# A decoder trunk on one core: MLA's mask and maximum in one VectorE operation, heads spawned ahead of values, words for transposes, a block's eight transposes in one run

## The chip, the core and the metric

The kernel runs on one core of a Trainium2 chip. Its engines work in parallel, each through its own list of instructions: TensorE (PE, matrix products and transposes), VectorE (DVE), ScalarE (ACT), GpSimd (POOL) and SyncE (SP, which issues DMAs). A product's stationary operand is loaded by an instruction of its own (LDWEIGHTS, shown as PEld). [...] The metric is the time of one execution on the device in microseconds, the median of several runs.

## What is computed

A decoder trunk of two layers over 256 positions and a width of 2048, all in float32. Layer 0 mixes with Mamba-2 heads (SSD) and, beside them, 16 heads of latent attention (MLA); layer 1 with stick-breaking attention. After each mixer comes a SwiGLU FFN with 5632 hidden columns, ahead of each sub-layer and at the end an RMSNorm. Most of the change is in MLA:

```python
q = (rms_norm(c_q, q_norm) @ w_uq).reshape(bsz, seq, 16, 128 + 64)
kv = (rms_norm(c_kv, kv_norm) @ w_ukv).reshape(bsz, seq, 16, 128 + 128)
q_nope, q_pe = jnp.split(q, [128], axis=-1)
k_nope, v = jnp.split(kv, [128], axis=-1)
q_pe, k_pe = apply_rope(q_pe, ...), apply_rope(k_rope, ...)
for i in range(2):                       # blocks of 128 query rows
    q0, q1 = i * 128, (i + 1) * 128
    s = (q_nope[q0:q1] @ k_nope[:q1].T + q_pe[q0:q1] @ k_pe[:q1].T) * scale   # per head
    mask = jnp.arange(q1)[None, :] <= jnp.arange(q0, q1)[:, None]
    p = jax.nn.softmax(jnp.where(mask, s, -jnp.inf), axis=-1)
    outs.append(p @ v[:q1])              # per head
```

The Mamba-2 part first runs a causal convolution of four taps with silu over 3072 channels; its outputs feed the scan.

## The kernel before

**Words.** Every float32 operand of a large product is split into two parts in a format that the code calls words (type F32R, 32 bits): ACT casts the high part (L346), DVE subtracts it from the source for the low part (L352), and three products (L460, L462, L463; L905 in the large ones) replace one. In the large layers the products are formed by a scheme of sums of weight blocks: DVE forms differences of weight tiles (L852) in two slots named wsum, and they too are split. Weights stay in SBUF in 12 slots of 8 KB a partition: four wh, six w, two wsum.

**Transposes.** An operand must have its channels on the partitions, so blocks of 128x128 are transposed on PE with an identity as the other operand. `transpose` (L352 to L359) takes `ident_r` if the source is a tile of words, and `ident` if it is f32. The same memory often has two names, one of each type: `twins` (raw and words), `xres` and `xwords` for the residual. Each transpose writes to a PSUM buffer named tr; there are four of them, and four of the accumulators acc. A block of 512 columns has eight transposes (four column tiles, two row tiles); `transpose_split` (L361) and `transpose_plain` (L388) do them in two runs of four into one tr buffer each, one step of the task apart.

**Order.** The order on PE is that of the written code. Beside the projections run tasks: Python generators, of which `yield n` says that the task sleeps for n ticks. A tick comes after each step of a projection's inner loop (a weight row block in both row tiles, six products), and resumes at most two tasks that are due. So a task's instructions stand on PE between products of the running projection. The order on ACT, DVE and POOL is made by a scheduler from priorities: `URGENT` (50000) ahead of the splitting of weights, whose numbers grow as the program goes on.

**MLA.** `mla_group` handles four heads, four times: the rotary part of the queries `qp` (24 products 256 wide), `q` and `k` transposed (48 products 256 wide each), `v` (24 products 512 wide), and then spawns four `mla_head` tasks with first waits of 2, 6, 10 and 14 ticks. A head computes its scores for the two blocks of rows (L1649, L1650) and adds a causal mask by a third product, `identb` with `cmask`, in bf16 (L1651); the scores are in one PSUM buffer `sc` (named at in the profile), 128 columns for the first block of rows and 256 for the second. DVE finds the maximum of each (L1656) and scales it by -scale (L1657); ACT takes the exponent with its sum (L1659); DVE forms the reciprocal (L1661) and scales the probabilities `p` (L1663). Seven ticks after the scores PE transposes three blocks of p (L1667, f32), ACT copies them (L1669), and four ticks later PE forms the output (L1673, L1674).

**Convolution and residual.** `conv` transposes the projected channels, applies the taps on DVE (L1502) and silu on ACT (L1504); four of its six tiles are the scan's x, which is transposed back at L1562. `norm_block` transposes the residual's column blocks j for the next operand; its rank says where it belongs: 100000 and above is the opening of the kernel, 99600 the first block of the last product's end, `URGENT` the blocks that `norm_next` calls.

## Time and profile before

| what | value |
|---|---|
| time, median of 3 runs | 2367.17 us (2367.09 to 2367.3) |
| the profiled execution, whole | 2367.28 us |
| its span in the profile | 2365.2 us |
| TensorE's granted clock in the profiled execution | 0.998 |
| transposes in words of twins | 352 on PE, 39.2 us |
| transposes in words of the residual | 88, 9.7 us |
| f32 transposes: p of MLA, residual, convolution | 48, 7.9 us; 40, 6.4 us; 32, 5.0 us |
| mask products of MLA | 32, 7.0 us |

The span is what the profile covers; the whole execution is 2.1 us longer. The busy times of PE count each product until its end, and since products overlap in a pipeline the distance from one start to the next is shorter than the time of one: busy times of a group on PE are not what the group would cost. A row of a timeline has the start in us, the time until the end of the last of its instructions, the engine, the line, the operation, output and inputs by the program's names, shapes, the count (x4 for four alike in a row), and in brackets the idle time ahead of it and what ended it.

### The profile page before, as it was taken

Reading aid. Unit: us, or ns where it says so; the run is one execution under the profiler, and the core shown is the slowest. Engines: PE = TensorE matmul, PEld = TensorE weight load, DVE = VectorE, ACT = ScalarE, POOL = GpSimd, SP = SyncE. Lnnn points to the kernel's source line nnn. Section 1 sums busy time; section 2 is a strip of 40 time slices with the busy share of each in tenths; the row PEclk is TensorE's granted clock in tenths of the full one; section 3 lists DMA queues with packets and bytes.
Section 4 is the critical chain, followed back from the end, with each engine's and each line's share of the span. In section 5 each row is a group of like instructions: output and inputs, shape, how many; then the busy total and the mean of one; then the engine's idle time right before and its main releaser. Section 6 shows DMA issues by size and latency. Waiting matters only on the chain.

```text
span 2365.2 us, 28220 instructions
## 1 busy us (share of the span) xinstructions
PE 2349.3 (99%) x11082; PEld 1953.9 (83%) x11082; DVE 2001.6 (85%) x1657; ACT 1467.2 (62%) x1486; POOL 215.7 (9%) x273
## 2 busy tenths in 40 slices
PE   9999999999999999999999999999999999999998
PEld 7888888988888888888888888888888888888886
DVE  6776587589998889989887898889997988989895
ACT  6655565566665655566665786776664656556664
POOL 1342001110000000000000020110000000000011
PEclk9999999999999999999999999999999999999999
DMA  7665556445666777777776555557667777767773
GB/s 273 204 194 179 184 196 188 135 142 195 231 203 207 225 217 215 223 219 221 218 241 207 203 182 176 185 175 242 226 203 213 216 228 221 217 214 228 216 253 110
DMA packets 271428, 486.33 MB, mean 206 GB/s; under 512 B 22268, under 2 KB 47488, under 8 KB 271296
## 3 DMA queue, kind: packets, MB, share of 16 engines
q1 hardware_dynamic: 255200, 445.95, 57.3%
q0 software_dynamic: 15232, 37.01, 6.5%
q8 instruction: 87, 1.43, 0.2%
q10 hardware_dynamic: 864, 1.57, 0.2%
q14 instruction: 45, 0.37, 0.0%
HBM read 459.24 MB, written 25.20 MB: 205 GB/s over the span
## 4 chain that ended last, share of the span: by engine, by line
PE 95%; DVE 2%; ACT 2%; issue 1%; DMA 0%; SPq 0%; ACTq 0%; DVEq 0%
PE acc L905 54%; PE acc L460 11%; PE acc L463 11%; PE acc L462 11%; PE tr L357 1%; PE acc L643 1%; PE acc L508 1%; ACT wh L346 1%; PE at L1578 1%; PE acc L510 0%; DVE wsum L852 0%; DVE wsum L352 0%; DVE w L352 0%; PE at L1649 0%; DMA xres<-in_x_dram 0%
## 5 line engine op out<-in xcount | busy, mean ns | idle before, releaser
L352 DVE TENSOR_TENSOR w<-w,wh 128x2048 fp32r<-128x2048 f32 (+2 forms) x399 | 893.4, 2246 | 174.8 <-ACT wh L346 168.4
L905 PE MATMUL acc<-wh,s 128*128 128x512 f32 x3896 | 985.4, 391 | 1.6 <-ACT s L926 1.2
L346 ACT CAST wh<-w 128x2048 fp32r<-128x2048 f32 (+2 forms) x399 | 744.5, 1874 | 322.9 <-PE acc L463 135.3
L905 PEld LDWEIGHTS acc<-wh,s 128*128 128x128 f32 x3896 | 725.5, 188 | 151.0 <-ACT s L926 1.7
L460 PE MATMUL acc<-wh,s 128*128 128x512 f32 (+1 forms) x1168 | 463.4, 397 | 0.1
L463 PE MATMUL acc<-wh,s 128*128 128x512 f32 (+1 forms) x1168 | 452.4, 387 | 0.2 <-DVE s L381 0.2
L462 PE MATMUL acc<-w,s 128*128 128x512 f32 (+1 forms) x1104 | 426.7, 387 | 0.0
L905 PE MATMUL acc<-w,s 128*128 128x512 f32 x1312 | 355.6, 389 | 0.2 <-DVE w L352 0.2
L905 PEld LDWEIGHTS acc<-w,s 128*128 128x128 f32 x1312 | 246.2, 188 | 52.1 <-DVE w L352 0.6
L463 PEld LDWEIGHTS acc<-wh,s 128*128 128x128 f32 x1168 | 219.3, 188 | 46.1 <-DVE s L381 0.6
L460 PEld LDWEIGHTS acc<-wh,s 128*128 128x128 f32 x1168 | 219.4, 188 | 43.6 <-issue 1.7
L462 PEld LDWEIGHTS acc<-w,s 128*128 128x128 f32 x1104 | 207.7, 188 | 40.0 <-issue 1.4
L352 DVE TENSOR_TENSOR wsum<-wsum,wh 128x2048 fp32r<-128x2048 f32 (+1 forms) x103 | 222.1, 2156 | 3.4 <-ACT wh L346 3.3
L346 ACT CAST wh<-wsum 128x2048 fp32r<-128x2048 f32 (+1 forms) x103 | 185.8, 1804 | 57.5 <-PE acc L905 38.4
L1067 POOL DMA_DIRECT2D saved<-s x64 | 55.9, 996 | 1107.0 <-ACT s L1066 1105.8
L346 ACT CAST wh<-lent 128x2048 fp32r<-128x2048 f32 (+1 forms) x62 | 114.6, 1858 | 62.4 <-DMA lent<-in_w_gate_dram 26.0
L352 DVE TENSOR_TENSOR lent<-lent,wh 128x2048 fp32r<-128x2048 f32 (+1 forms) x62 | 137.1, 2217 | 11.6 <-ACT wh L346 11.1
L852 DVE TENSOR_TENSOR wsum<-w,wsum 128x2048 f32<-128x2048 f32 (+1 forms) x54 | 106.7, 1976 | 19.2 <-PE acc L905 16.6
L905 PE MATMUL acc<-wsum,s 128*128 128x512 f32 x380 | 104.6, 390 | 1.4 <-DVE wsum L352 1.4
L905 PEld LDWEIGHTS acc<-wsum,s 128*128 128x128 f32 x380 | 71.2, 188 | 17.1 <-DVE wsum L352 2.2
L926 ACT COPY s<-acc 128x512 f32<-128x512 f32 x88 | 51.6, 588 | 39.1 <-PE acc L905 39.1
L852 DVE TENSOR_TENSOR wsum<-w,w 128x2048 f32<-128x2048 f32 (+1 forms) x36 | 72.6, 2017 | 1.7 <-DMA w<-in_w_qkv_dram 1.7
(280 smaller groups left out, 1966.8 us busy)
## 6 DMA issues: line engine op xcount, KB each, us to landing
w<-in_w_down_dram SPq DMA_DIRECT2D x80, 1024.0 KB, 4.9
w<-in_w_gate_dram SPq DMA_DIRECT2D x76, 1024.0 KB, 5.1
w<-in_w_up_dram SPq DMA_DIRECT2D x76, 1024.0 KB, 5.1
w<-in_w_qkv_dram SPq DMA_DIRECT2D x48, 1024.0 KB, 5.0
w<-in_w_in_dram SPq DMA_DIRECT2D x45, 1024.0 KB, 5.1
w<-in_w_out_even_dram SPq DMA_DIRECT2D x32, 1024.0 KB, 4.9
saved<-s POOLq DMA_DIRECT2D x64, 256.0 KB, 7.3
w<-in_w_out_odd_dram SPq DMA_DIRECT2D x16, 1024.0 KB, 5.0
```

Of the source, the lines that this page charges most:

```text
L346: cast = nc.scalar.copy(hi, src).ins
L352: return nc.vector.tensor_tensor(lo, src, hi.bitcast(F32), op=ALU.subtract).ins
L357: self.nc.tensor.transpose(out.bitcast(F32R), src, self.ident_r)
L460: nc.tensor.matmul(ps[t], hi[:, ts], wh, start=k == 0, stop=False)
L462: slot.used(nc.tensor.matmul(ps[t], hi[:, ts], wl, start=False, stop=False), self.clock)
L463: nc.tensor.matmul(ps[t], lo[:, ts], wh, start=False, stop=k == nk - 1)
L508: nc.tensor.matmul(ps[:, h % 2], wh[:, hs], x, start=k == n == 0, stop=False)
L643: m = nc.tensor.matmul(ps[b], x, y, start=b not in started, stop=stop, skip_group_check=True)
L852: ins = self.nc.vector.tensor_tensor(half(o, so), half(p, sp), half(q, sq), op=ALU.subtract).ins
L905: m = nc.tensor.matmul(ps[b], x, y, start=b not in started, stop=stop, skip_group_check=True)
L926: copied = nc.scalar.copy(o, ps[b]).ins
L1067: nc.gpsimd.dma_start(self.saved[n][:, t], s, accum_op=ALU.add)
```

## The change

The change has four parts.

1. **Mask and maximum.** The product with `identb` and `cmask` is dropped, and so are these two constants (another tile, `more_filler`, takes their space). POOL builds a mask tile in SBUF once, ahead of the four groups: 128 columns of zeros and 128 of the triangle. `tensor_tensor_reduce` on DVE reads scores and mask, adds them, multiplies by -scale, writes the result back into `sc`, and leaves the minimum in `mx`. Two such operations replace the two reduces and the scaling; the exponent is then taken with a scale of -1.
2. **Heads ahead of values.** The four heads are spawned ahead of the projection of `v`, and `v` is a list that it fills. The waits inside a head go from 7 and 4 ticks to 5 and 3.
3. **Words for transposes.** Eight tiles of 512 columns are laid over the two wsum slots under two names, `lease` (f32) and `leasewords`. The convolution's first four tiles and the probabilities of 11 of the 16 heads (the groups 0 and 1, and three heads of group 2) live there, and are transposed as words. The residual's blocks of `norm_next` use `xwords` (only rank 99600 stays with f32).
4. **One run of eight.** A block's eight transposes are written in one run into two tr buffers, taken at once, in `transpose_split` (but not at the opening), in `transpose_plain` and in a block of the operand.

```diff
     def transpose_split(self, src, res, g=None, wait=3, rank=None):
 
+        pts = []
         for k2 in range(2):
-            yield wait if k2 == 0 else 1
-            pt = self.tr([2, S])
-            for k in range(2):
-                for t in range(2):
-                    self.transpose(pt[:, k, t * P:(t + 1) * P], src(t, 2 * k2 + k))
+            if k2 == 0 or rank and rank > 50000:
+                yield wait if k2 == 0 else 1
+            if k2 == len(pts):
+                for n in range(k2, 1 if rank and rank > 50000 and k2 == 0 else 2):
+                    pts.append(self.tr([2, S]))
+                    for k in range(2):
+                        for t in range(2):
+                            self.transpose(pts[n][:, k, t * P:(t + 1) * P], src(t, 2 * n + k))
+            pt = pts[k2]
...
     def norm_block(self, st, j, g, wait=2, rank=None, blocks=False, spill=None, pause=2):
-        x = (self.xres if rank and rank < 100000 else self.xwords)[j]
+        x = (self.xres if rank == 99600 else self.xwords)[j]
...
         oT = self.operand()
+        self.mask = self.s2([2 * P])
+        nc.gpsimd.memset(self.mask, 0.0)
+        nc.gpsimd.affine_select(self.mask[:, P:], self.mask[:, P:], [[-1, P]], ALU.is_ge, NEG, base=0,
+                                channel_multiplier=1)
...
-            o = self.s2([2, S])
-            res.append(o)
+            if n < 4:
+                o, w = (a.rearrange("p (k s) -> p k s", k=2) for a in self.lease(2 * n + k2))
+                res.append(w)
+            else:
+                o = self.s2([2, S])
+                res.append(o)
...
-                nc.tensor.transpose(pt[:, k * P:(k + 1) * P], xT[k // 2][:, k % 2, t * P:(t + 1) * P], self.ident)
+                self.transpose(pt[:, k * P:(k + 1) * P], xT[k // 2][:, k % 2, t * P:(t + 1) * P])
...
-        v = self.evac(self.project(ckv, heads(wkv, 128, 128), 4))
+        v = []
         o, left = self.out_tiles(g), [0, 1, 2, 3]
...
         oT["xT"].append((self.spawn(self.wait_all(tasks)), o))
+        v += self.evac(self.project(ckv, heads(wkv, 128, 128), 4))
...
-            nc.tensor.matmul(dst, qpT[:, q0:q1], self.kpeT[:, h % 2, 0:ks], start=False, stop=False)
-            nc.tensor.matmul(dst[:, ks - P:ks], self.identb, self.cmask, start=False, stop=True)
+            nc.tensor.matmul(dst, qpT[:, q0:q1], self.kpeT[:, h % 2, 0:ks], start=False, stop=True)
         mx, sm = self.small([P, 2], "mx"), self.small([P, 2], "sm")
-        p = self.s2([3 * P])
+        if g < 2 or g == 2 and h < 3:
+            p, words = (a[:, :3 * P] for a in self.lease(4 * (g > 0) + h))
+        else:
+            p = words = self.s2([3 * P])
         regs = (slice(0, P), slice(P, 3 * P))
         for t in range(2):
-            nc.vector.tensor_reduce(mx[:, t:t + 1], sc[:, regs[t]], AX.X, ALU.max)
-        nc.vector.tensor_scalar(mx, mx, -scale, None, op0=ALU.mult)
+            nc.vector.tensor_tensor_reduce(sc[:, regs[t]], sc[:, regs[t]], self.mask[:, P * (1 - t):], -scale, -NEG,
+                                           ALU.add, ALU.min, mx[:, t:t + 1])
         for t in range(2):
-            nc.scalar.activation(p[:, regs[t]], sc[:, regs[t]], AF.Exp, scale=scale, bias=mx[:, t:t + 1],
+            nc.scalar.activation(p[:, regs[t]], sc[:, regs[t]], AF.Exp, scale=-1.0, bias=mx[:, t:t + 1],
                                  accum_out=sm[:, t:t + 1])
...
-        yield 7
+        yield 5
         pt = self.tr([3 * P])
         for b in range(3):
-            nc.tensor.transpose(pt[:, b * P:(b + 1) * P], p[:, b * P:(b + 1) * P], self.ident)
+            self.transpose(pt[:, b * P:(b + 1) * P], words[:, b * P:(b + 1) * P])
         pT = self.s2([3 * P])
         nc.scalar.copy(pT, pt)
-        yield 4
+        yield 3
```

The rows below stand in the order of the built programs. Line numbers of the kernel after are larger: L352 and L359 are now L355 and L362, L357 is L360, L460 to L463 are L469 to L472, L852 is L862, L905 is L915, L1649 and L1650 are L1668 and L1669.

On PE, the scores of the first MLA head. Before, they stand in the next group's query projection (256 wide), each pair of products followed by the mask's:

```order
L463 MATMUL acc_3280<-wh_67,s_201_1855 128x256
L1649 MATMUL at_3299<-s_303_3205,s_299_3145 128x128
L1650 MATMUL at_3299<-kpeT,s_306_3225 128x128
L1651 LDWEIGHTS identb
L1651 MATMUL at_3299<-cmask,identb 128x128
L1649 MATMUL at_3299<-s_303_3205,s_299_3145 128x256
L1650 MATMUL at_3299<-kpeT,s_306_3225 128x256
```

Now they stand in the middle of the same group's projection of v (512 wide), without the mask:

```order
L472 MATMUL acc_3247<-wh_66,s_212_2035 128x512
L1668 MATMUL at_3266<-s_295_3208,s_291_3148 128x128
L1669 MATMUL at_3266<-kpeT,s_298_3228 128x128
L1668 MATMUL at_3266<-s_295_3208,s_291_3148 128x256
L1669 MATMUL at_3266<-kpeT,s_298_3228 128x256
L469 MATMUL acc_3246<-wh_66,s_213_2040 128x512
```

The mask's two products and their weight loads are gone, and the head comes a projection earlier.

On DVE, the second head of the third group, whose rows are mixed with the splitting of weights (w, wsum and wh are weight tiles). Before:

```order
L352 TENSOR_TENSOR w_73<-w_74,wh_66 128x2048
L1656 TENSOR_REDUCE mx_3948<-at_3941 128x1 x2
L852 TENSOR_TENSOR wsum_82<-w_80,w_76 128x2048
L1657 TENSOR_SCALAR mx_3948<-mx_3948 128x2
L352 TENSOR_TENSOR w_75<-w_76,wh_67 128x2048
L1661 RECIPROCAL sm_3949<-sm_3949 128x2
L1663 TENSOR_SCALAR s_411_3950<-s_411_3950,sm_3949 128x128
L1663 TENSOR_SCALAR s_411_3950<-s_411_3950,sm_3949 128x256
```

Now:

```order
L355 TENSOR_TENSOR w_73<-w_74,wh_66 128x2048
L1677 ISA at_3947,mx_3952<-at_3947,s_286_3065 128x128
L1677 ISA mx_3952 128x1
L862 TENSOR_TENSOR wsum_82<-w_80,w_76 128x2048
L1677 ISA at_3947,mx_3952<-at_3947,s_286_3065 128x256
L1677 ISA mx_3952 128x1
L355 TENSOR_TENSOR w_75<-w_76,wh_67 128x2048
L1682 RECIPROCAL sm_3953<-sm_3953 128x2
```

The three rows of reduces and scaling have become four rows of the new operation, and the difference of weights that stood between the reduces and the scaling now stands between the two minima.

On PE, the residual's third block in layer 0, whose transposes stand between the products of the output projection. Before, in f32 and in two runs:

```order
L905 MATMUL acc_4961<-w_71,s_535_4811 128x512 x4
L359 MATMUL tr_4980<-ident,xres_87 128x128 x4
L905 MATMUL acc_4962<-wh_66,s_541_4843 128x512
L905 MATMUL acc_4962<-wh_66,s_542_4844 128x512
L905 MATMUL acc_4962<-wh_66,s_541_4843 128x512
L905 MATMUL acc_4962<-wh_66,s_542_4844 128x512
L359 MATMUL tr_4999<-ident,xres_87 128x128 x4
L905 MATMUL acc_4962<-wh_66,s_541_4843 128x512
```

After, the same block is in words and in one run:

```order
L915 MATMUL acc_4905<-w_71,s_516_4747 128x512 x4
L360 MATMUL tr_4924<-ident_r,xwords_91 128x128 x4
L360 MATMUL tr_4929<-ident_r,xwords_91 128x128 x4
L915 MATMUL acc_4906<-wh_66,s_522_4781 128x512
L915 MATMUL acc_4906<-wh_66,s_523_4782 128x512
L915 MATMUL acc_4906<-wh_66,s_522_4781 128x512
```

The four products that stood between the two runs now stand behind both.

More of the change, by code (lines that the diff above doesn't have):

```diff
@@ L161, in weight_slots @@
                       for t in range(4)]
+        first = self.HIGH + self.LOW
+        lease = lambda k, name, dt: nc.alloc_sbuf_tensor_at(
+            f"{name}{k}", [P, 512], dt, offset=base + 8192 * first + 2048 * k).ap()
+        self.leases = [Twin(lease(k, "lease", F32), lease(k, "leasewords", F32R)) for k in range(8)]
         self.saved = [self.dp.tile([P, 2, 512], F32, name=f"saved{j}") for j in range(4)]
@@ L169, in weight_slots, with lease @@
         self.spare = [at(f"spare{q}", [P, 512], q) for q in range(8)]
+    def lease(self, k):
+        return self.leases[k].raw, self.leases[k].words
     def wsum(self):
@@ L277, in constant_tiles @@
         nc.gpsimd.dma_start(self.ident_r.bitcast(F32), self.ident)
-        self.identb = c([P, P], "identb", BF16)
-        make_identity(nc, self.identb)
         ones = self.s2([P])
@@ L290, in constant_tiles @@
         self.ones = self.ones_r.bitcast(F32)
-        zero = self.s2([P])
-        nc.gpsimd.memset(zero, 0.0)
-        self.cmask = c([P, P], "cmask", BF16)
-        nc.gpsimd.affine_select(self.cmask, zero, [[-1, P]], ALU.is_ge, NEG, base=0, channel_multiplier=1)
+        c([P, P], "more_filler")
         self.vm, self.va, self.vb = c([P, 32], "vm"), c([P, 56], "va"), c([P, 120], "vb")
@@ L388, in transpose_plain @@
     def transpose_plain(self, src, res, wait=4):
-        for k2 in range(2):
-            yield wait if k2 == 0 else 1
-            pt = self.tr([2, S])
+        yield wait
+        pts = [self.tr([2, S]) for _ in range(2)]
+        for k2, pt in enumerate(pts):
             for k in range(2):
@@ L395, in transpose_plain @@
                     self.transpose(pt[:, k, t * P:(t + 1) * P], src(t, 2 * k2 + k))
+        for pt in pts:
             o = self.s2([2, S])
@@ L776, in gen @@
             res = []
-            for t in range(2):
-                yield first if t == 0 else 1
-                pt = self.tr([4, P])
+            yield first
+            pts = [self.tr([4, P]) for _ in range(2)]
+            for t, pt in enumerate(pts):
                 for k in range(4):
                     self.transpose(pt[:, k], src(t, k))
+            for pt in pts:
                 r = self.s2([4, P])
```

## The prediction

> **What bounds the kernel now.** I read the page's head and its chain first, then TensorE's (PE's) waits between 20 and 2360 us, then busy time in four stretches.
>
> ```profile
> span 2365.2 us, 28220 instructions
> PE 2349.3 (99%) x11082; PEld 1953.9 (83%) x11082; DVE 2001.6 (85%) x1657; ACT 1467.2 (62%) x1486; POOL 215.7 (9%) x273
> PE 95%; DVE 2%; ACT 2%; issue 1%; DMA 0%; SPq 0%; ACTq 0%; DVEq 0%
> PE acc L905 <- DVE wsum L352: 1.4, 2, 0.7
> PE acc L905 <- ACT s L926: 1.2, 1, 1.2
> PE at L1518 <- ACT s L1504: 0.6, 1, 0.6
> PE tr L1562 <- ACT s L1504: 0.5, 1, 0.5
> 470.00:515.00 45.00, 45.00 (x299) 40.83 (x299) 33.69 (x55) 25.95 (x57) 10.44 (x12) 1.00 0.42 142
> 555.00:626.00 71.00, 70.22 (x326) 57.54 (x325) 70.85 (x65) 44.97 (x54) 2.21 (x4) 1.00 0.66 225
> 1614.00:1686.00 72.00, 71.27 (x332) 58.78 (x331) 71.30 (x64) 46.70 (x55) 2.15 (x4) 1.00 0.67 225
> 640.00:1290.00 650.00, 650.00 (x2932) 537.99 (x2931) 574.88 (x373) 389.14 (x317) 31.74 (x39) 1.00 0.70 218
> ```
>
> PE is busy for 99% of the span and holds 95% of the chain. The wait rows (total, times, longest) add up to 3.7 us. In a stretch the columns are length, then busy time and count of PE, weight loads, VectorE (DVE), ScalarE (ACT) and GpSimd (POOL), then the granted clock. From 640 to 1290 PE isn't idle at all, at a clock of 1.00; so a PE instruction taken out there shortens the kernel by the time that it held PE. Only at the two FFN entries (555 to 626, 1614 to 1686) is DVE as full as PE: 70.85 of 71 us, 71.30 of 72. DMA is busy for 0.42 to 0.70 of these stretches and the change issues no transfer, so I leave it out.
>
> The sum is made against the profiled execution, 2367.28 us: its span of 2365.2 and 2.1 around it. The median of the three runs shown is 2367.17, 0.1 lower.
>
> **The mask: 16 x 0.14 = 2.2 us off PE.** A head's scores in the timeline (start, duration, instruction):
>
> ```profile
> 422.81 0.39 PE L1650 MATMUL at<-kpeT,s 128*128 128x128 f32 x2
> 423.03 0.22 PE L1651 MATMUL at<-cmask,identb 128*128 128x128 bf16 x1
> 423.08 0.65 PE L1649 MATMUL at<-s,s 128*128 128x256 f32 x2
> 423.57 0.59 PE L1650 MATMUL at<-kpeT,s 128*128 128x256 f32 x2
> 424.00 0.22 PE L1651 MATMUL at<-cmask,identb 128*128 128x128 bf16 x1
> 424.03 0.36 PE L460 MATMUL acc<-wh,s 128*128 128x256 f32 x1
> ```
>
> Ends overlap in a pipeline, so what an instruction costs is the distance to the next start. The mask's two products cost 0.05 and 0.03; and the pair behind the first takes 0.49 (423.08 to 423.57) where the next pair takes 0.43 (to 424.00), which I put down to the refill after a short bf16 product: 0.06. Together 0.14 per head, 2.2 us for 16 heads.
>
> On DVE two reduces and a scaling become two masked minima:
>
> ```profile
> 446.23 0.62 DVE L1656 TENSOR_REDUCE mx<-at 128x1 f32<-128x128 f32 x2 [0.51 <-PE at L1651]
> 446.89 0.17 DVE L1657 TENSOR_SCALAR mx<-mx 128x2 f32<-128x2 f32 x1
> 130.03 2.04 DVE L1502 SCALAR_TENSOR_TENSOR s<-tr,vb,s 128x255 f32<-128x255 f32 x5
> 447.89 0.20 ACT L1659 ACTIVATION_READ_ACCUMULATOR s<-at,mx 128x1 f32 x1
> ```
>
> No row shows the new operation. It can't be cheaper than the two reduces, since it reads the same scores: 0.62 a head, 0.17 under today's 0.62 + 0.17. From above: L1502 reads PSUM and SBUF and writes 255 wide in 0.41 (2.04 / 5); two of these, each with an accumulator read as ACT's at 0.20, make 1.22, 0.43 over today. I take the upper end, whose operands are nearest: 16 x 0.43 = 7 us more DVE work in MLA. It is hidden: from 470 to 515 DVE has 33.69 of 45 us in use and PE waits for nothing. Without that cover the price is at most 7 us.
>
> **Words instead of f32 for 97 transposes: 2.0 us off PE.** A run of four of each kind, with the products behind it, then two runs of eight:
>
> ```profile
> 111.28 0.60 PE L1562 MATMUL tr<-ident,s 128*128 128x128 f32 x4
> 111.64 0.48 PE L460 MATMUL acc<-wh,s 128*128 128x512 f32 x1
> 111.96 0.39 PE L462 MATMUL acc<-w,s 128*128 128x512 f32 x1
> ...
> 114.94 0.46 PE L357 MATMUL tr<-ident_r,twinwords 128*128 128x128 f32 x4
> 115.24 0.46 PE L460 MATMUL acc<-wh,s 128*128 128x512 f32 x1
> 115.54 0.39 PE L462 MATMUL acc<-w,s 128*128 128x512 f32 x1
> 115.77 0.39 PE L463 MATMUL acc<-wh,s 128*128 128x512 f32 x1
> ...
> 1344.94 1.07 PE L905 MATMUL acc<-wsum,s 128*128 128x512 f32 x4
> 1345.85 0.79 PE L357 MATMUL tr<-ident_r,twinwords 128*128 128x128 f32 x8
> 1346.48 1.18 PE L905 MATMUL acc<-wh,s 128*128 128x512 f32 x4
> 1347.49 0.79 PE L357 MATMUL tr<-ident_r,twinwords 128*128 128x128 f32 x8
> ```
>
> Four f32 transposes and two products behind them take 0.91 (111.28 to 112.19), of which undisturbed products would be 2 x 0.23 (115.54 to 115.77): the run costs 0.45, of which 0.36 is the run and 0.09 a refill of the product behind. In words the same stretch (114.94 to 115.77) takes 0.83: the run costs 0.37, again with a refill. Later products lose 0.01 to 0.02 more, so I put 0.46 and 0.39: a run of four gains 0.07 to 0.08. A run of eight in words is 0.63 (1345.85 to 1346.48), and the four products behind it take 1.01 instead of the 0.91 of the four ahead of it: 0.73.
>
> - Convolution: 32 transposes at L1562, 8 runs x 0.077 = 0.6.
> - Probabilities: 11 of the 16 heads get a leased tile, the other 5 stay f32. A run of three is 0.75 of a run of four, 11 x 0.055 = 0.6.
> - The residual's blocks n=2 and 3 in both layers (L359, 32 transposes), words and merged at once: eight f32 runs at 0.46 become four runs of eight at 0.73: 3.7 - 2.9 = 0.8.
>
> The leased tiles lie in the two wsum slots, which DVE builds again only behind the users of the lease; this adds a wait only if a head is late.
>
> A rule speaks for more. The Trainium skill's "FP8 and Floating Point Precision", section "TensorE Precision Notes", has true FP32 take four passes through the PE array and reduced-precision FP32 one. By it a run of four in words would cost, as an estimate, a quarter of 0.36, 0.09, not 0.30; the trace disagrees for transposes as short as these.
>
> **One run of eight instead of two of four: 38 x 0.05 = 1.9 us.** Two runs of four at 0.39 are 0.78, one of eight 0.73. The order has 42 fewer runs of transposes, four of them the residual's, already counted. Both PSUM tiles are now taken at once; there are four such buffers, and behind each block stand over ten products, 2.3 us, before the next asks.
>
> **Stalls.** Two of the wait rows are the convolution's. Its transposes waited 0.5 for ACT at L1504 (the 0.6 at L1518 stays); in the new order their operands come before other ACT work: -0.5. L905's 1.2 behind the copy at L926: this copy stands behind a head's, which now come earlier: -0.4. L905's two waits for wsum L352: the DVE order now builds the differences earlier at the second, -0.45, and -0.2 at the first. Against this stands that at the FFN entries DVE has no room: what PE gains from the residual's transposes there (0.8) it waits for wsum again; I charge 0.65. And I charge 0.5 for new waits in MLA. Together -0.4.
>
> **Heads ahead of values, waits 7 to 5 and 4 to 3: nothing.** The same products, in another order. From scores to transposes PE had 72 products of 256 (half of 0.23: 8.5 us) and the next scores. Now the first head has some 12 of 512, 18 of 256 and the next head's scores (1.2): 2.8 + 2.1 + 1.2 = 6.1 us; the others 7 to 9. What must fit is the chain maximum, exp, reciprocal, scaling. Where DVE is free it ends with this, 2.9 us after the scores (445.97):
>
> ```profile
> 445.97 0.22 PE L1651 MATMUL at<-cmask,identb 128*128 128x128 bf16 x1
> 448.12 0.17 DVE L1661 RECIPROCAL sm<-sm 128x2 f32<-128x2 f32 x1 [1.06 <-ACT s L1659]
> 448.32 0.55 DVE L1663 TENSOR_SCALAR s<-s,sm 128x128 f32<-128x128 f32 x2
> 489.84 0.22 PE L1651 MATMUL at<-cmask,identb 128*128 128x128 bf16 x1
> 492.35 0.61 DVE L1656 TENSOR_REDUCE mx<-at 128x1 f32<-128x128 f32 x2
> 492.88 2.43 DVE L852 TENSOR_TENSOR w<-w,w 128x2048 f32<-128x2048 f32 x1
> 498.65 0.74 DVE L1663 TENSOR_SCALAR s<-s,sm 128x128 f32<-128x128 f32 x2
> ```
>
> and with weight differences of 2.4 us ahead of and between its steps it ends at 499.39, 9.5 us after the scores (489.87). A head like that would be late by 0.5 to 2.5 us at a distance of 7 to 9; in the new order no L852 difference stands inside the chain of the first nine heads. I take one such wait of 0.5 (charged above); the bounds are 0 and four of 1.5, 6 us. Behind a waiting transpose stand all of PE's later products, so each microsecond counts in full.
>
> **Sum:** 2.2 + 2.0 + 1.9 + 0.4 = 6.5 us; 2367.28 - 6.5 = 2360.8, against the median 2360.7.
>
> **The rivals.**
>
> *Part of it comes back.* The FFN entries are DVE's, and two or three heads wait: 2360.7 + 0.2 for the rest of the residual's gain + 2.6 for two heads at 1.3 = 2363.5. For it: DVE at 70.85 of 71, and the 9.5 us of the chain behind 489.87. Against it: at 446 the chain took 2.9.
>
> *Every short stall goes.* The four wait rows vanish (-3.7 instead of -1.55) and nothing new comes: 2360.7 - 2.2 - 0.5 = 2358.0. For it: the waits are short, and each is behind ACT or DVE work that the order moves; against it: 640 to 1290 shows that PE takes what it is offered, the entries that DVE sets the pace.
>
> *Words cost a quarter of f32.* If the leased tiles and all runs of words were that cheap, the 19 f32 runs and the residual's eight would gain about 0.27 each where I have some 0.07, 27 x 0.2 = 5 more: about 2355.5. The rule cited above says so; the row at 114.94 (0.30 for four in words) speaks against it.
>
> *Slower: the masked minimum is long, and the heads wait.* The mechanism is the chain of a head: the minimum stands between scores and exp, twice a head, and writes the scores back to PSUM before exp may read. If it takes 1.5 us or more instead of 0.41, a chain like that of 489.87 goes from 9.5 past 11 us against a distance of 7 to 9, and heads wait 2 us each. It turns the sign when the heads together wait 7 us, that is 16 heads at 0.45 or 6 at 1.2. With 6 heads at 2 us: 2360.7 + 12 = 2372. For it: the operation isn't in the trace, and the order shows it as two rows. "VectorE: DVE Perf Modes" of the Trainium skill, section "Two Vector instructions with no wait between them", has an operation that writes out its accumulator as two instructions; only the trace after can show their length. Against it: L1502's 0.41 with the same operands.
>
> *The change doesn't do what it says.* The order shows the mask's products gone and the runs merged, so only the sizes are open.
>
> **Chances.** Forecast 0.55 (2359.3 to 2362.4), comes back 0.24, stalls gone 0.12, cheap words 0.03, slower 0.06. A measurement of this kernel can tell about 0.2%, 4.7 us, from no change, so faster means under 2362.4: 0.55 + 0.12 + 0.03 = 0.70; same 0.24; slower 0.06. The range leaves out the slow and the cheap case and some 0.06 of the tails: 2357.8 to 2364.8.
>
> **What would show it.** PE's instructions fewer by 32, and no bf16 product in the heads. Runs of eight at 0.63 and 66 runs of transposes instead of 108. L1562's form with words at 0.24 a transpose instead of 0.27. No PE wait for a head's probabilities longer than 0.5; a row "PE tr <- DVE" of several microseconds, with the new minimum over 1 us, would make the slower rival right. PE's busy time lower by 6 us and its waits by 0.4; waits for wsum of more than 1.4 in total would be the gain come back.

## The result, and the profile after

| | median | lowest to highest | runs |
|---|---|---|---|
| before | 2367.17 us | 2366.99 to 2367.30 | 5 |
| after | 2382.26 us | 2380.61 to 2386.11 | 5 |

The ratio is 1.0066, with a 95% interval of 1.0053 to 1.0079: 15.1 us slower, outside the range. The times of the kernel after also scatter over 5.5 us, those of before over 0.3. The profiled execution took 2386.11 us, the longest of the five.

The head of the page and its chain:

```profile
span 2384.4 us, 28170 instructions
PE 2353.2 (99%) x11050; PEld 1958.6 (82%) x11050; DVE 2004.2 (84%) x1673; ACT 1469.1 (62%) x1486; POOL 217.8 (9%) x271
PE 91%; DVE 5%; issue 1%; ACT 1%; DMA 1%; SPq 0%; DVEq 0%; ACTq 0%
```

The 32 products of the mask are gone (11050 instead of 11082). Yet PE's busy time went up by 4 us, and its share of the chain fell from 95 to 91%, with DVE now at 5%. The first rows of PE's waits (line, who ended the wait, us in total, times, longest):

```profile
PE at L1260 <- DVE s L406: 5.7, 3, 1.9
PE at L1669 <- DVE s L1654: 5.4, 1, 5.4
PE at L1694 <- ACT s L1690: 4.0, 2, 2.3
PE tr L360 <- DMA xres<-in_x_dram: 2.2, 1, 2.2
```

Of these four, before has only the last, at 0.6 us; its waits of the middle came to 3.7 us. The four add up to 17.3 us. That a wait also makes PE busier is seen in busy times by stretch (columns as in the prediction; the clock granted stands after POOL). Three stretches of after, each right behind a wait:

```profile
492.90:497.00 4.10, 4.02 (x17) 3.61 (x18) 4.10 (x6) 2.37 (x7) 3.21 (x4) 0.64 0.00 0
519.20:524.00 4.80, 4.74 (x12) 3.82 (x13) 1.43 (x8) 0.91 (x4) 0.00 (x0) 0.50 0.00 0
1359.70:1364.00 4.30, 4.30 (x14) 3.48 (x15) 4.30 (x3) 2.82 (x4) 0.00 (x0) 0.65 0.00 0
```

The clock is at half for a while, and PE does the same work in more time. The clock records of the trace have six such stretches ahead of the end, the first in the opening, of 3.4 us, 3.4, 6.8, 3.4, 3.4 and 3.4, all at 0.5, each at a wait of 1.87 us or more. Before has none ahead of its end. At half clock 3.4 us cost 1.7 us of work.

Where the time went is read by setting the start of the same weight product in both traces side by side (an ordinary list; 9870 such products in each):

```
program                      start before   after minus before
opening, behind block 2          17 us          +3.8 us
convolution and scan done       282             +2.4
MLA begins                      418             +2.5
MLA's last heads                517            +16.5
first FFN entered               668            +10.3
stick-breaking begins          1344             +9.6
stick-breaking ends            1573            +20.4
last product                   2356            +19.0
```

So there are three places of loss: the opening (3.8), MLA (14, of which 6 come back until 668, partly because the heads now stand ahead of products that they stood behind), and stick-breaking (10.8). Elsewhere the kernel gains: 1.4 up to 282, 1.4 behind 1573. In stick-breaking the account closes: 5.7 us of waits and three stretches at half clock, 1.7 each, are 10.8.

### The profile page after: what moved, and what is told of

It reads as the page before. It is cut to its first block, busy times and chain, and to the rows that moved or that the text cites. A ratio compares the mean times of both kernels' runs of the same rounds, so it can differ in the third digit from the quotient of the medians.

```text
span 2384.4 us, 28170 instructions
## 1 busy us (share of the span) xinstructions
PE 2353.2 (99%) x11050; PEld 1958.6 (82%) x11050; DVE 2004.2 (84%) x1673; ACT 1469.1 (62%) x1486; POOL 217.8 (9%) x271
## 3 DMA queue, kind: packets, MB, share of 16 engines
q8 instruction: 87, 1.43, 0.2%
## 4 chain that ended last, share of the span: by engine, by line
PE 91%; DVE 5%; issue 1%; ACT 1%; DMA 1%; SPq 0%; DVEq 0%; ACTq 0%
PE acc L915 51%; PE acc L469 11%; PE acc L472 11%; PE acc L471 11%; PE tr L360 1%; PE acc L652 1%; PE acc L517 1%; DVE w L355 1%; DVE wsum L862 1%; DVE wsum L355 1%; PE at L1596 1%; ACT wh L349 1%; PE acc L519 0%; DMA xres<-in_x_dram 0%; PE at L1669 0%
## 5 line engine op out<-in xcount | busy, mean ns | idle before, releaser
L355 DVE TENSOR_TENSOR w<-w,wh 128x2048 fp32r<-128x2048 f32 (+2 forms) x399 | 893.6, 2246 | 175.6 <-ACT wh L349 166.0
L915 PE MATMUL acc<-wh,s 128*128 128x512 f32 x3896 | 981.2, 391 | 1.0 <-ACT s L936 0.7
L915 PEld LDWEIGHTS acc<-wh,s 128*128 128x128 f32 x3896 | 727.9, 188 | 151.0 <-ACT s L936 1.1
L469 PE MATMUL acc<-wh,s 128*128 128x512 f32 (+1 forms) x1168 | 463.5, 397 | 0.1
L472 PE MATMUL acc<-wh,s 128*128 128x512 f32 (+1 forms) x1168 | 453.2, 388 | 0.2 <-DVE s L389 0.2
L915 PE MATMUL acc<-w,s 128*128 128x512 f32 x1312 | 357.3, 391 | 0.2 <-DVE w L355 0.2
L915 PEld LDWEIGHTS acc<-w,s 128*128 128x128 f32 x1312 | 247.5, 189 | 52.5 <-DVE w L355 0.6
L472 PEld LDWEIGHTS acc<-wh,s 128*128 128x128 f32 x1168 | 219.9, 188 | 46.1 <-DVE s L389 0.6
L469 PEld LDWEIGHTS acc<-wh,s 128*128 128x128 f32 x1168 | 220.2, 188 | 44.1 <-issue 1.7
L355 DVE TENSOR_TENSOR wsum<-wsum,wh 128x2048 fp32r<-128x2048 f32 (+1 forms) x103 | 222.0, 2155 | 16.1 <-ACT wh L349 16.1
L355 DVE TENSOR_TENSOR lent<-lent,wh 128x2048 fp32r<-128x2048 f32 (+1 forms) x62 | 137.0, 2216 | 12.1 <-ACT wh L349 11.8
L862 DVE TENSOR_TENSOR wsum<-w,wsum 128x2048 f32<-128x2048 f32 (+1 forms) x54 | 106.4, 1971 | 21.5 <-PE acc L915 17.2
L915 PE MATMUL acc<-wsum,s 128*128 128x512 f32 x380 | 104.5, 390 | 0.3 <-DVE wsum L355 0.3
L915 PEld LDWEIGHTS acc<-wsum,s 128*128 128x128 f32 x380 | 71.2, 188 | 16.0 <-DVE wsum L355 1.2
L862 DVE TENSOR_TENSOR wsum<-w,w 128x2048 f32<-128x2048 f32 (+1 forms) x36 | 72.5, 2015 | 2.9 <-DMA w<-in_w_qkv_dram 1.8
```

The costliest lines, as they stand in the source:

```text
L355: return nc.vector.tensor_tensor(lo, src, hi.bitcast(F32), op=ALU.subtract).ins
L469: nc.tensor.matmul(ps[t], hi[:, ts], wh, start=k == 0, stop=False)
L472: nc.tensor.matmul(ps[t], lo[:, ts], wh, start=False, stop=k == nk - 1)
L862: ins = self.nc.vector.tensor_tensor(half(o, so), half(p, sp), half(q, sq), op=ALU.subtract).ins
L915: m = nc.tensor.matmul(ps[b], x, y, start=b not in started, stop=stop, skip_group_check=True)
```

## The experiments

Line numbers of the experiments shift by a few from those of the kernel after. All times are medians, with the ratio to runs of the kernel before on the same chip and its 95% interval; before was between 2367.10 and 2367.24 in each group.

### First: undoing one order at a time

Theory at this point: the short waits and the early heads make MLA wait, the merge in `transpose_plain` makes stick-breaking wait. Rivals: a lower clock or the masked minimum.

**e1_plain_two.** `transpose_plain` in two runs again:

```diff
-        yield wait
-        pts = [self.tr([2, S]) for _ in range(2)]
-        for k2, pt in enumerate(pts):
+        for k2 in range(2):
+            yield wait if k2 == 0 else 1
+            pt = self.tr([2, S])
...
-        for pt in pts:
```

> The changed kernel, but with the q and k blocks of stick-breaking (transpose_plain) transposed in two runs of four a tick apart, as before. Theory A (the merge lets the score task of stick-breaking start one tick earlier, so that PE asks for the copies at L406 some 2 us before DVE has made them, three times, and each wait of about 1.9 us is followed by some 4 us at about half the granted clock): the three waits L1260 <- DVE L406 vanish, 3 x 3.6 = 10.9 us less, about 2371.3. Theory B (the loss is spread: a noisy opening, a lower clock, slower transposes in words): the waits may go but the time stays above 2379.

Measured: 2373.01 us, 1.0024 (1.0014 to 1.0034). The three waits are gone, 9.3 us less. The rows that explain them, of the kernel after on PE and on DVE:

```profile
1355.32 1.47 PE L360 MATMUL tr<-ident_r,twinwords 128*128 128x128 f32 x16
1356.62 1.16 PE L915 MATMUL acc<-wh,s 128*128 128x512 f32 x4
1359.70 0.70 PE L1260 MATMUL at<-s,s 128*128 128x256 f32 x2 [1.92 <-DVE s L406]
...
1355.57 2.28 DVE L862 TENSOR_TENSOR wsum<-w,wsum 128x2048 f32<-128x2048 f32 x1
1357.77 2.48 DVE L406 COPY s<-tr 128x512 f32<-128x512 f32 x4
```

and the same place before:

```profile
1350.03 0.59 PE L1250 MATMUL at<-s,s 128*128 128x256 f32 x2
...
1346.10 2.28 DVE L852 TENSOR_TENSOR wsum<-w,wsum 128x2048 f32<-128x2048 f32 x1
1348.30 2.48 DVE L397 COPY s<-tr 128x512 f32<-128x512 f32 x4
```

DVE does the same in both: a difference of weights, then four copies. But before, the 16 transposes of a q and a k block took two ticks, each tick's two places being full, so that `stick_weights` came a tick later: its scores started at 1350.03, 1.9 us after the second run ended (1348.12). Now the 16 stand in one tick, and the scores are due four products later, at 1357.78 (1359.70 less the wait of 1.92), when the copies are just beginning (1357.77).

**e4_stick6.** The merge stays, and `stick_weights` sleeps one tick more:

```diff
-        yield 5
+        yield 6
```

> The changed kernel with one number changed: stick_weights sleeps 6 ticks instead of 5 ahead of its scores, so the scores stand where the two half runs had put them; the merge stays. Theory A (the tick): the three waits at L1260 vanish, about 2371, as in e1. Rival C (the merge itself: two tr buffers taken at once, so that the copies at L406 come late whatever the tick): the waits stay near 1.9 us, about 2382.

Measured: 2375.11 us, 1.0032 (1.0020 to 1.0044): 7.2 us less than the kernel after. Two of the three waits are gone, the third is 1.6 us. So the tick does it, though not to the full.

**e2_mla_order and e3_both.** Heads behind v, waits 7 and 4; in e3 also `transpose_plain` in two runs:

```diff
-        v = []
+        v = self.evac(self.project(ckv, heads(wkv, 128, 128), 4))
...
-        v += self.evac(self.project(ckv, heads(wkv, 128, 128), 4))
...
-        yield 5
+        yield 7
...
-        yield 3
+        yield 4
```

> The changed kernel, but with MLA's heads spawned behind the projection of v and with the waits 7 and 4, as before; mask on VectorE and words stay. Theory A (the shorter waits bring the output product within four ticks of the next head's scores, and ScalarE's copy of the transposed probabilities is queued behind the next head's exponents; heads ahead of v ask for the rotary copy L1654 before it is made): the waits L1694 <- ACT L1690 and L1669 <- DVE L1654 vanish, 9.3 us that MLA lost in the trace and 1 to 2 more that mask and words gain: 2382.3 - 11 = 2371.3. Theory B (the new masked minimum makes the heads late whatever the order): the waits stay or move to the transposes of the probabilities, time above 2379.

> The changed kernel without both orders: transpose_plain in two runs, heads behind v, waits 7 and 4. What is left of the change: mask and minimum on VectorE, words for 97 transposes, merged runs in transpose_split and in the operand's blocks. Theory A: nothing waits more than before, and PE keeps what the prediction counted, less the merges of transpose_plain: 2367.2 - 6 = 2361 (2359.5 to 2363). Theory B: clock or slower instructions remain, over 2366.

Measured: e2 2378.01 us, 1.0044 (1.0032 to 1.0057); e3 2369.09 us, 1.0008 (1.0000 to 1.0017). The waits of MLA vanish, but two others come at its end, 3.1 us behind a copy of an accumulator on ACT and 3.3 behind DVE. Theory A missed both times by 7 to 8 us: something else in the change did not fit the old order.

### Second: single parts

**f1_identb.** e3 with the unused constant kept:

```diff
+        self.identb = c([P, P], "identb", BF16)
+        make_identity(nc, self.identb)
...
-        c([P, P], "more_filler")
+        c([P, P], "more_filler", BF16)
```

> e3 with the constant identb kept, though nothing reads it: its memset and selection put the DMA of dt_bias on GpSimd's queue back behind the loads of the norms (at 5.6 us as before, instead of 1.35). Theory A (that DMA, issued at 1.35, holds up the second residual block in the opening: 2.2 us of waiting instead of 0.6): the wait is back at 0.6, 1.5 to 3 us less than e3, about 2367, and the spread of the times narrows from 2.3 us to under 1.5. Rival (the opening's load is late for another reason, or by chance): same as e3, 2369.1, with its spread.

Measured: 2367.57 us, 1.0001 (0.9993 to 1.0010), 1.5 us less than e3. On POOL the kernel after has

```profile
1.35 0.71 POOL L268 DMA_DIRECT2D hp<-in_dt_bias_dram  x1 [0.34 <-issue]
12.53 0.59 PE L360 MATMUL tr<-ident_r,xwords 128*128 128x128 f32 x4 [2.23 <-DMA xres<-in_x_dram]
```

(the second row is PE), where before had

```profile
5.61 0.57 POOL L260 DMA_DIRECT2D hp<-in_dt_bias_dram  x1
10.39 0.50 PE L357 MATMUL tr<-ident_r,xwords 128*128 128x128 f32 x4 [0.64 <-DMA xres<-in_x_dram]
```

With a memset and a selection less, the scheduler moved a DMA of POOL to the front, and the residual's second block landed later. f1 has that DMA at 5.59 us again and a wait of 0.5 us for the block, where e3 has 1.35 and 2.2. That it is this DMA which delays the block is argued: no run moves it alone.

**f2_words_merge.** Words and merges alone (e3, with the mask on TensorE again and its constants):

```diff
+            nc.tensor.matmul(dst[:, ks - P:ks], self.identb, self.cmask, start=False, stop=True)
...
+            nc.vector.tensor_reduce(mx[:, t:t + 1], sc[:, regs[t]], AX.X, ALU.max)
+        nc.vector.tensor_scalar(mx, mx, -scale, None, op0=ALU.mult)
```

> Words and merged runs alone: the mask and the maximum as before (products on TensorE, two reduces, identb and cmask kept), heads behind v, waits 7 and 4, transpose_plain in two runs; so the leases, xwords and the merges of transpose_split and of the operand's blocks are what differs from before. Theory A (the waits of 3.1 and 3.3 us at the end of MLA in e3 come from the masked minimum, whose two halves the DVE order sets apart with weight differences between): these waits vanish, and the time is 2367.2 - 0.6 - 0.6 - 0.8 - 1.5 = 2363.7 (2362.5 to 2364.5). Rival (they come from the leases, which hold the wsum slots longer): the waits stay, 2367 or more.

Measured: 2370.72 us, 1.0015 (1.0006 to 1.0024). The rival: the waits at MLA's end stay without the masked minimum. PE and DVE of f2 there:

```profile
522.99 1.65 PE L920 MATMUL acc<-wh,s 128*128 128x512 f32 x3 [3.27 <-DVE s L361]
...
517.25 2.28 DVE L867 TENSOR_TENSOR wsum<-w,wsum 128x2048 f32<-128x2048 f32 x1
519.45 2.28 DVE L361 TENSOR_TENSOR wsum<-wsum,wh 128x2048 fp32r<-128x2048 f32 x1
521.65 1.28 DVE L361 TENSOR_TENSOR s<-s,s 128x512 fp32r<-128x512 f32 x2
```

Before had there:

```profile
516.67 1.29 DVE L352 TENSOR_TENSOR s<-s,s 128x512 fp32r<-128x512 f32 x2 [0.93 <-ACT s L346]
517.88 2.28 DVE L852 TENSOR_TENSOR wsum<-w,wsum 128x2048 f32<-128x2048 f32 x1
520.16 2.27 DVE L352 TENSOR_TENSOR wsum<-wsum,wh 128x2048 fp32r<-128x2048 f32 x1
```

The operand's low parts (s<-s,s) stand behind two operations on wsum in f2, and ahead of them before. The rival holds: the masked minimum is not the cause.

**f3_mask_alone.** The kernel before with the masked minimum only (f2's edit the other way round, constants kept).

> The kernel before with the masked minimum alone: the 32 products with cmask are gone, the mask tile and the two masked minima a head are in, constants, order, transposes as before. Theory A (the minimum itself takes 0.3 to 0.4 us a half, but weight differences of 2.3 us come between the halves, and MLA's end waits for them): 2.2 us of products less, 5 or more of waits more, about 2370. Theory of the prediction (DVE has room): 2365.

Measured: 2367.28 us, 0.9999 (0.9990 to 1.0008), between both. In its trace PE gains 2.2 us on before from 418 to 491 us, as the mask's products were worth, and then loses them again:

```profile
500.45 0.54 PE L357 MATMUL tr<-ident_r,twinwords 128*128 128x128 f32 x4 [2.73 <-POOL twin L1486]
...
488.92 2.50 POOL L1482 TENSOR_TENSOR twin<-ropea,ropeb 128x128 f32<-128x128 f32 x1
...
496.95 0.51 POOL L1482 TENSOR_TENSOR twin<-ropea,ropeb 128x128 f32<-128x128 f32 x1
...
488.56 2.54 DVE L852 TENSOR_TENSOR wsum<-w,wsum 128x2048 f32<-128x2048 f32 x1
```

Before, PE did not wait for the rotary products on POOL. Here the same operation takes 0.51 us at 496.95 and 2.50 at 488.92, beside DVE's operation on 2048 columns.

**f4_heads_ahead.** f2 with heads ahead of v and the waits 5 and 3.

> Words and merged runs as in f2, and the heads ahead of v with the waits 5 and 3, but the mask on TensorE as before. Theory A (the shorter waits and the earlier heads make PE ask before ACT and DVE have made the copies, whatever the mask): two waits at the output product behind ScalarE's copy of p, and one at the scores behind the rotary copy, 8 us or more over f2. Rival (only the masked minimum makes them late): as f2 within 1 us.

Measured: 2373.75 us, 1.0027 (1.0017 to 1.0037), 3.0 over f2, where 8 or more were expected. The three waits of the kernel after are there (4.1 and 3.6 us), with the mask on TensorE: the masked minimum is not their cause. f2 has waits of 3.1 and 3.3 us at MLA's end that f4 does not have, so the 3.0 are less than what the three waits cost.

### Third: the leases of the probabilities

The order of DVE, which is known without a run, has, with the heads behind v, the two operations on wsum ahead of the operand's low parts only if `p` is leased. So the next four set `p` on tiles of its own, or do that alone.

```diff
-        if g < 2 or g == 2 and h < 3:
-            p, words = (a[:, :3 * P] for a in self.lease(4 * (g > 0) + h))
-        else:
-            p = words = self.s2([3 * P])
+        p = words = self.s2([3 * P])
```

**g3_no_p** is f2 with this edit, **g7_p_only** the kernel before with the leases of `p` alone, **h1_no_p_mask_dve** is g3 with the masked minimum, **h2_rope8** is h1 with the rotary transposes a tick later (`yield 8` for 7).

> f2 without the leases of the probabilities: they are f32 tiles of their own as before, so the leases of the convolution, xwords and the merges of transpose_split and of the operand's blocks are what differs from before. Theory A (the leases of the probabilities in the wsum slots make the scheduler set two builds of wsum ahead of the operand's low parts and of the head's scaling on DVE at MLA's end): the waits of 3.1 and 3.3 us vanish, and with them the slow clock behind them: 2370.7 - 8 + 0.6 = 2363.3 (2362.5 to 2364.5). Rival (merges or the convolution's leases do it): 2370.

> The kernel before with one thing: the probabilities of 11 heads live in the wsum slots and are transposed as words (convolution and residual as before, no merges, mask on TensorE). Theory A: the two waits at MLA's end appear, 8 us with the slow clock, less 0.6 of words: about 2374. Rival: 2366.6.

> g3 with the masked minimum on VectorE (identb kept for GpSimd's order). Theory A: the mask gains 2.2 us of products, and PE then comes to the rotary transposes of the last group before GpSimd has made them, as in f3 (2.7 us of waiting): as g3 or up to 0.6 better, 2362.5 to 2363.5. Theory of the prediction (all of it is a gain): 2361.2.

> h1 with the rotary transposes one tick later (8 instead of 7), 1.4 us. Theory A (the wait is for GpSimd's rotary products, whose own duration goes from 0.5 to 2.5 us beside a wide VectorE operation): the wait drops from 2.7 to about 1.3 or nothing, 1.5 us or more less than h1, about 2361.3.

Measured: g3 2363.79 us, 0.9986 (0.9977 to 0.9995); g7 2373.86, 1.0029 (1.0017 to 1.0040); h1 2364.11, 0.9987 (0.9978 to 0.9995); h2 2361.35, 0.9975 (0.9966 to 0.9985). Theory A held: g3 came 0.5 us over its 2363.3, g7 and h2 within 0.2 us, h1 0.6 above the upper end of its range. PE's wait for POOL is 2.6 us in h1 and 1.3 in h2. With the old order of the heads and the mask on TensorE, the leases of `p` cost 6.6 to 6.9 us (g7 against before, f2 against g3); words for the convolution, xwords and the merges gain 3.4.

### Fourth: which order, on a kernel without the other waits

**i2_waits53** is h2 with the waits 5 and 3, **i3_heads_ahead** is h1 with the heads ahead of v, **i4_no_identb** is h2 without the constant, **i5_plain_merged** is h2 with the merge in `transpose_plain`.

> h2 with the waits inside a head shortened from 7 and 4 to 5 and 3 ticks, heads still behind v. Theory A (between the next head's scores and a head's output product stand 4 ticks instead of 7, some 5.8 us, and ScalarE's copy of the transposed probabilities is queued behind the next head's exponents, whose chain takes up to 8 us): one or two waits at the output product behind that copy, 2 us each and as much again in slow clock, 2361.4 + 3 to 8: 2366. Rival (only heads ahead of v matters): 2361.4.

> h1 (rotary transposes at 7) with the heads spawned ahead of the projection of v, waits 7 and 4. Theory A (the first head's scores come 24 products earlier, 5.5 us, and the rotary copy on VectorE, which is behind weight differences, is not there): a wait at the scores behind the rotary copy of 3 to 5 us with its slow clock; h1 2364.1 + 3 to 7: 2369. Rival (only the short waits matter): 2362 to 2364.5, the rotary wait on GpSimd included.

> h2 without the constant identb: one memset and one selection less on GpSimd, and the DMA of dt_bias is issued second there, at 1.35 us. Theory A (it takes DMA time from the second residual block): the wait for that block goes from 1.2 to 2 us or more, 2361.4 + 1 to 3: 2363.4, with a wider spread. Rival (nothing): 2361.4.

> h2 with transpose_plain in one run of eight, stick_weights at 5 ticks as in the change. Theory A: three waits of 1.9 us at L1260's scores behind the copies at L406, with the slow clock 3.6 each: 2361.4 + 10.9 = 2372.3. Rival (the three waits belong to other parts of the change): 2361.

Measured: i2 2410.03 us, 1.0180 (1.0166 to 1.0193); i3 2360.02, 0.9971 (0.9960 to 0.9982); i4 2362.23, 0.9980 (0.9972 to 0.9989); i5 2370.28, 1.0013 (1.0004 to 1.0022).

i4 adds 0.9 us; its wait for the residual's block is 1.5 us, against 1.2 in h2. Its wider spread (2.5 against 1.3) is one execution of eleven. i5 adds 8.9: the three waits of 1.9 us are there. i3 refutes theory A: heads ahead of v make no new wait; they gain 4.1 us over h1, some of it because the rotary wait on POOL falls from 2.6 to 1.4 us. i2 missed altogether. Its 49 us come from waits in both FFNs and in stick-breaking, where the orders of DVE and ACT differ from h2's though nothing was edited there; why the scheduler chose them is open, so i2's time does not price the short waits. In MLA itself it is level with h2: from 418 to 601 us both gain 2.7 us on before, i2 with a wait of 1.0 at an output product. So the runs show a loss from the short waits in MLA only together with the heads ahead of v.

**j1_no_p_53** is i3 with the waits 5 and 3, **j2_p_74** is i3 with the leases of `p`. Far from MLA the orders of both are those of i3.

> i3 with the short waits, 5 and 3: all of the change but the leases of the probabilities, the merge in transpose_plain and the loss of identb. Theory P (the three waits inside MLA come from the leases of the probabilities, which make the scheduler put weight builds between the steps of a head): none of these waits, 2360 to 2361.5. Rival W (they come from the short waits together with the heads ahead of v, as first thought): two waits at the output product behind ScalarE's copy, 2365 or more.

> i3 with the leases of the probabilities: heads ahead of v, waits 7 and 4. Theory P: waits of 3 us or more come back in the third and fourth group, 2366 to 2372. Rival W: as i3, less 0.6 of words, 2359.5.

Measured: j1 2372.00 us, 1.0020 (1.0011 to 1.0029); j2 2357.97, 0.9961 (0.9948 to 0.9973). Theory P fell. Rival W has the right pair of edits and the wrong place: j1 waits 6.2 us at the transposes of the probabilities, for their scaling on DVE, and 2.6 at the scores, behind the rotary copy, but only 0.6 at an output product. j2 came 1.5 us under the rival's 2359.5. The corners, in us (short waits with the heads behind v have no usable time, see i2):

| heads, waits | p on tiles of its own | p leased |
|---|---|---|
| behind v, 7 and 4 | 2364.1 (h1) | 2367.6 (f1) |
| ahead of v, 7 and 4 | 2360.0 (i3) | 2358.0 (j2) |
| ahead of v, 5 and 3 | 2372.0 (j1) | 2373.0 (e1, without identb) |

With the heads ahead of v, the short waits cost 12 us without the leases; with them 15.0, of which 0.9 to 1.5 are identb's (i4, f1). The leases cost only with the heads behind v (3.5 here, 6.6 to 6.9 with the mask on TensorE). j2 beats both kernels: 9.1 us faster than before, all its times within 0.6 us, and no stretch of half clock up to the end. Its span and PE's longest waits between 20 and 2350 us:

```profile
span 2356.7 us, 28163 instructions
PE acc L916 <- ACT s L937: 1.2, 1, 1.2
PE acc L916 <- DVE wsum L357: 0.7, 1, 0.7
PE at L1537 <- ACT s L1523: 0.6, 1, 0.6
```

The whole loss by these runs: j2's 2358.0, plus 15.0 for the short waits and identb (to e1), plus 9.3 for the merge in `transpose_plain`, is the 2382.3 of the kernel after. The same merge costs 8.9 on h2 (i5).

## How the short waits work

In the kernel after, the wait of 2.3 us at an output product (rows of PE, ACT and DVE):

```profile
486.65 0.37 PE L360 MATMUL tr<-ident_r,leasewords 128*128 128x128 f32 x3
492.98 0.70 PE L1694 MATMUL at<-s,s 128*128 128x256 f32 x2 [2.30 <-ACT s L1690]
...
491.64 0.37 ACT L1680 ACTIVATE lease<-at,mx 128x128 f32<-128x128 f32 x1 [1.89 <-DVE mx L1677]
492.45 0.48 ACT L1690 COPY s<-tr 128x384 f32<-128x384 f32 x1
...
488.85 2.29 DVE L862 TENSOR_TENSOR wsum<-w,w 128x2048 f32<-128x2048 f32 x1 [1.14 <-DMA w<-in_w_out_even_dram]
491.06 0.42 DVE L1677 CUSTOM_DVE_ANT_0 at<-at,s 128x256 f32<-128x256 f32 x1
```

The probabilities of one head were transposed at 486.65. Their copy (L1690) is behind the exponents of the next head on ACT, and these wait for the second minimum, which stands behind a difference of weights on DVE, which waits for its DMA. The copy comes at 492.45, 5.8 us after their start, and the output product is due four ticks behind the next head's scores. With 7 and 4 it is due seven ticks behind them.

The wait of 5.4 us is of the same kind, on another line:

```profile
509.74 0.45 PE L360 MATMUL tr<-ident_r,twinwords 128*128 128x128 f32 x4
519.26 0.80 PE L1669 MATMUL at<-kpeT,s 128*128 128x128 f32 x2 [5.38 <-DVE s L1654]
...
510.20 2.29 DVE L862 TENSOR_TENSOR wsum<-w,wsum 128x2048 f32<-128x2048 f32 x1
...
512.48 2.27 DVE L355 TENSOR_TENSOR wsum<-wsum,wh 128x2048 fp32r<-128x2048 f32 x1
...
515.73 2.28 DVE L355 TENSOR_TENSOR w<-w,wh 128x2048 fp32r<-128x2048 f32 x1
517.93 0.68 DVE L355 TENSOR_TENSOR s<-s,s 128x512 fp32r<-128x512 f32 x1
518.53 0.68 DVE L1654 COPY s<-tr 128x512 f32<-128x512 f32 x1
```

The rotary transposes end at 510.0, their copy comes 8.5 us later, behind three weight operations of 2.3 us. In j2 these transposes start at 497.76 and their copy at 500.86, ahead of the weight operations. The waits of the head do not stand between these two steps: that this wait belongs to the short waits is shown by i3 and j2, which do not have it, and not by these rows. In j1, without the leases, a third step is late too: the transposes that wait 6.2 us for the scaling. Which step is late depends on where the scheduler set the weight operations; that one is late is common to j1, e1 and f4, and none is in i3 and j2.

## Why the prediction was wrong

The gains were right where a run singles them out, and their sum was even too small: j2 gains 9.1 us where 6.5 were forecast, above all because heads ahead of v, which the prediction put at nothing, gain 4.1 with the old waits (i3 against h1). What failed is that the short waits were charged 0.5 us, that the merge in `transpose_plain` was counted as a gain, and that the opening was not seen.

- **Mask, 2.2 us: right.** h1 gains 2.2 us on before between 418 and 491 us of the trace, and g3, which has the mask on TensorE, nothing there. But with the heads behind v PE loses it again in waiting for POOL (2.7 us in f3, 2.6 in h1): f3 is level with before, h1 with g3, and only h2, a tick later, keeps it (2.4 us less than g3). The kernel after has no wait for POOL in its list.
- **The masked minimum, 1.22 us a head at most: right that it is hidden, too high.** The groups on DVE of after:

```profile
L1677 DVE CUSTOM_DVE_ANT_0 at<-at,s 128x256 f32<-128x256 f32 x16 | 6.9, 431 | 0.5
L1677 DVE CUSTOM_DVE_ANT_0 at<-at,s 128x128 f32<-128x128 f32 x16 | 4.7, 295 | 6.7 <-PE at L1669 6.4
L1677 DVE DVE_READ_ACCUMULATOR2_ANT mx<- 128x1 f32 x32 | 4.5, 141 | 0.0
```

  16.1 us for 16 heads, 1.0 a head. So the slower rival had the right mechanism, heads that are late, and the wrong cause: f4 has the waits without this operation.
- **Words, 2.0 us: right as far as shown.** Leased probabilities gain 0.65 in g7's trace from 418 to 517 us, ahead of its waits (0.6 predicted); the convolution gains 1.0 in g3's, its wait included (0.6 and 0.5 predicted). The residual's 0.8 was measured only together with the merges.
- **"One run of eight": right for `transpose_split`, wrong for `transpose_plain`.** A run of eight takes 0.62 us in after's trace (0.63 predicted), and words and merges without those of `transpose_plain` gain 3.4 in g3, where the terms of the prediction for them (0.6, 0.8, 34 x 0.05 and 0.5 of stalls) make 3.6. But I counted 38 merges at 0.05 and asked only whether PSUM, which holds the results of PE, has room. A merge also takes a tick out of the program: the task that waits for these blocks comes earlier, and DVE's copies do not. Four of the 38 merges, worth 0.2 us, cost 8.9 to 9.3.
- **"Heads ahead of values, waits 7 to 5 and 4 to 3: nothing": the step that failed most.** The prediction compared the distance from a head's scores to its own transposes (6 to 9 us) with the chain of 2.9 to 9.5, saw heads that would be late by up to 2.5 us, and charged 0.5, with a bound of 6. Measured, it is 12 us (j1 against i3), and 14 to 15 with the leases (e1 against j2, less identb's 0.9 to 1.5 from 15.0). Three things were missing: the copy behind the next head's exponents, whose distance is the one that shrank from seven ticks to four; the rotary copy; and the price of a wait. A wait of 2 us was put at 2 us, but behind it the clock is at half in some cases, which adds 1.7 us for every 3.4.
- **Stalls: the gains came, the charge of 0.65 at the FFN entries did not.** In after's list the convolution's wait of 0.5 is gone, that behind ACT's copy fell from 1.2 to 0.7, and those for wsum from 1.4 to 0.3. From 601 to 668 us after and j2 both gain 1.5 on before.
- **Not seen: POOL's order in the opening.** A constant less (identb) moved a DMA to the front of a queue: 0.9 to 1.5 us (i4, e3 against f1). The prediction spoke of the DMAs only to leave them out.

The Trainium skill's "TensorE: Matmul & The Clock Gate", section "Part 1: The HAM clock gate (the "warmup" mystery)", has the clock at half behind an idle window of about 3.4 us, and the window free-running. The trace agrees with the length: the low stretches are 3.4 us or multiples of it. The same page of the Trainium skill, section "Why this matters for your kernels", asks for no gap over about 3 us; here waits of 1.9 us were enough, though not each time.

## What to carry to other kernels

A wait counted in steps of the program (ticks, yields) is a promise on time: whoever shortens it, or merges two steps into one, must look at every engine in the chain behind it, and first at what stands in front of each operation in its queue, not at how long the operation takes. A merge that saves 0.05 us can take out a step that hid 2 us. And where a scheduler orders an engine, a removed constant or a shared buffer is an edit of the order: compare the queues, the opening's too, ahead of the times.

## What was not expected of the hardware

Equal waits are followed by different clocks. In i5, three waits of 1.92, 1.87 and 1.91 us on PE; the 3.4 us behind each of them (columns as above):

```profile
1345.90:1349.30 3.40, 3.40 (x17) 2.95 (x18) 3.40 (x3) 2.43 (x4) 0.00 (x0) 1.00 0.00 0
1395.30:1398.70 3.40, 3.40 (x12) 2.78 (x13) 3.40 (x3) 3.34 (x5) 0.00 (x0) 0.69 0.02 5
1492.60:1496.00 3.40, 3.40 (x17) 2.95 (x18) 3.40 (x3) 1.54 (x3) 0.00 (x0) 1.00 0.00 0
```

Only the second is slow, and does 12 products where the others do 17. In the kernel after all three were. Over all traces of this case PE has, behind its first products, 16 idle gaps of 1.71 to 1.93 us, and eight of them are followed by a stretch at half clock; of the gaps of 1.0 to 1.67 us none is.

The scatter goes with the clock. In the kernel after, the recorded mean clock is 0.994 in the run of 2386.11 us, 0.995 in those of 2384.05 and 2382.26, and 0.996 in those of 2380.89 and 2380.61; 0.002 of 2382 us is 4.8 us, of a scatter of 5.5. All this fits a window that runs on its own, so that it is left to the execution which short wait is followed by half clock. No run here sets the phase of that window, so this is argued, not shown. And it is not all: i3 scatters over 2.4 us, though its profiled execution, the fastest of seven, has no idle gap of PE over 1.43 us; its longer ones have no profile.
